# Causal squares of the row-maximum pass: a GpSimd select in place of a mask matmul

## The chip, the cores and the metric

One core of a Trainium2 chip runs the whole kernel. The metric is the device time of one execution in microseconds (us); the kernel before took 1416.82 us, the median of three runs. The engines are TensorE (PE; its weight loads are PEld), VectorE (DVE), ScalarE (ACT), GpSimd (POOL) and SyncE (SP), which here only issues DMAs. Each works through its own queue of instructions in order, and a wait at the head of a queue holds everything behind it.

## The reference, cut to what matters

One decoder layer over 2048 tokens of width 1024: `x + W_out(concat(A, B, C) * silu(z))`, where A is latent attention (8 heads), B differential attention (4 heads, two softmax maps each) and C attention to 256 memory tokens. A and B are causal:

```python
sc = jnp.einsum('bqhd,bkhd->bhqk', qblk, k).astype(jnp.float32) * scale
sc = jnp.where(causal_mask(start, s)[None, None], sc, NEG_INF)
p = jax.nn.softmax(sc, axis=-1)
```

A softmax may subtract any number near the row's maximum before the exponential, since it cancels in the quotient. The kernel computes a row maximum of the masked scores beforehand and carries it into the scores as one more row of the contraction.

## The kernel before, in words

The 2048 queries are cut into 4 blocks of 512 (b = 0 to 3), each of 4 row tiles of 128. The work is a list of 28 steps: 4 of the memory branch, 8 of the differential branch (2 groups of heads x 4 blocks), 16 of the latent branch (4 groups x 4 blocks). A step has a preparation (`prep_d`, `prep_a`: projections, norms and rotary embedding, keys and queries split into fp16 pairs and transposed by DMA), then the row-maximum pass `est_block`, then its maps (class `Map`): for each tile of 128 keys the scores with keys on the partitions (L546, or L890 to L892, with a mask product at L549 or L894 for the diagonal tile), the exponential p on ACT (L492), the low part plo on DVE (L493), and the products with the values on PE (L502, L504, L505).

`est_block` (L373) is where the change is. For each map m, row tile t and key block c up to b it makes on PE the scores of 128 queries (on the partitions) against up to 512 keys (L384, tile pe, one of three PSUM banks). In the query's own block, c == b, only the first t + 1 squares of 128 keys are computed, and the last of these, on the diagonal, gets the causal mask by a second product at L386, identity times `mask_e`, which adds -1e30 above the diagonal into the same bank. How the maximum is then taken depends on `fold`, true for b of 1 or more:

- Block 0: DVE reduces the bank directly (L388, tile mx).
- Blocks 1 to 3: ACT copies the first key block from PSUM to a bf16 tile er (L390; one buffer, holding two row tiles) and each later one to a bf16 tile ec (L393; three buffers). DVE takes the elementwise maximum of er and ec (L394). After each pair of row tiles DVE halves er three times (L398) and reduces the rest (L399).

Then DVE writes the scaled maxima into the query stack (L407), and SP issues the DMA that transposes the queries again with the maxima in them (L470, L873), which releases the maps. In blocks 1 to 3 the diagonal square always passes through an ec, never through er.

POOL, beside the memsets of the stacks (L448, L853, L859), computes the norms: an addition (L97) and a power of -1/2 (L101, tiles r_d, r_a, yr_d), the rotary tables (L318 to L321), and in the latent branch the rotary embedding of the queries (L340 to L344), the last of which DVE's L845 and L848 need. POOL issues one DMA, at the start; all others are SP's.

A loop at the end of the kernel (from L1176) decides in which order steps, fills (gates, latents, output projection) and maps are written down, from planned costs and due times; preparation and `est_block` get a priority 200 behind that of the maps. The tile framework then makes each engine's queue from these priorities and a modelled timeline, anew at each build:

```python
with tile.TileContext(nc, schedule_with_timeline_sim=True) as tc:
```

Of the kernel before, what the change touches and what calls it, by code (L numbers as in the profile page):

```python
# [16 lines left out]
ALU = mybir.AluOpType  # L17
AX = mybir.AxisListType

P = 128  # L20
# [4 lines left out]
NK = DM // P  # L25
EPS = 1e-6
NEG = -1.0e30
WS = 64.0
# [12 lines left out]
def hybrid_block(ctx: ExitStack, tc: tile.TileContext, x, mem, positions, norm_g, w_in, mla_q_norm_g,  # L41
# [3 lines left out]
    V, A, G, T, SP = nc.vector, nc.scalar, nc.gpsimd, nc.tensor, nc.sync  # L45
# [15 lines left out]
    def bigt(shape, name):  # L61
        return big.tile(shape, F16, tag="big", name=name)

# [1 line left out]
    ident = cst.tile([P, P], BF16, name="ident")  # L65
    make_identity(nc, ident)
    mask_t = cst.tile([P, P], BF16, name="mask_t")
# [33 lines left out]
        G.tensor_tensor(rv, rv, m.broadcast_to([P] + list(shape)), ALU.pow)  # L101
        return rv

# [1 line left out]
    def stage(name, pool=None):  # L105
        if pool is big:
            return big.tile([P, DM], F32, tag="big", name=name)
# [6 lines left out]
    PACE, NPACE = 6, 6  # L114

    def load(dst, src, pace=PACE):
        """At the start, loads take turns with the transposes on the DMA queues."""
        if 0 < len(turned) < 2 * NPACE:
            with tc.issue_after(turned[max(0, len(turned) - pace)].ins):
                SP.dma_start(dst, src)  # L120
        else:
            SP.dma_start(dst, src)
# [16 lines left out]
        turned.append(SP.dma_start_transpose(ht[:, 1], lo))  # L139
        return ht  # L140

# [1 line left out]
    def load_w(w, cols, gains, name, out, pool=None, ahead=2, pace=PACE):  # L143
        """Column ranges of w as fp16 pairs: NK views [P, 2, n] appended to out."""
        n = sum(c for _, c in cols)
        kpu = 2 if n > 256 else 4

        def fetch(i):
            st = stage(f"wst_{name}{i}", pool).rearrange("p (k c) -> p k c", k=2)
            at = 0  # L150
            for c0, c in cols:
                load(st[:, :, at:at + c], w[0, 2 * i * P:(2 * i + 2) * P, c0:c0 + c].rearrange("(k p) c -> p k c", p=P), pace)
                at += c
            return st

        sts = [fetch(i) for i in range(ahead - 1)]
        yield 1.0
        for i in range(NK // 2):
            if i + ahead - 1 < NK // 2:
                sts.append(fetch(i + ahead - 1))  # L160
                yield 1.0
            st = sts[i]
            if 2 * i % kpu == 0:
                wt = bigt([P, kpu, 2, 1024 // kpu], f"w_{name}{i}")
            for k in range(2):
                g = gains[:, 2 * i + k:2 * i + k + 1]
                dst = wt[:, (2 * i + k) % kpu]
                A.activation(dst[:, 0, :n], st[:, k, :n], AF.Copy, scale=g)
                V.scalar_tensor_tensor(dst[:, 1, :n], st[:, k, :n], g, dst[:, 0, :n], ALU.mult, ALU.subtract)
                out.append(dst)  # L170
            yield 1.0
# [6 lines left out]
            T.matmul(ps[:, :n], lhsT=ht[:, 1, k], rhs=wt[:, 0, :n], start=False, stop=(k == NK - 1))  # L178

    def project_block(hts, units, n, dst):  # L180
        """dst: [P, 4, >= n]"""
        for t in range(4):
            ps = ps_p.tile([P, 512], F32, tag="pp", name="pp")
            project(ps, hts[t], units, n)
            A.activation(dst[:, t, 0:n], ps[:, :n], AF.Copy, scale=1.0 / WS)
            yield 0.01 * n
# [4 lines left out]
    def tmp4(name):  # L191
        return wk.tile([P, 1024], F32, tag="t4", name=name, bufs=2)

# [1 line left out]
    top = tc.cur_priority  # L195
    tc.cur_priority = top + 1000
    g_mk = gain_row(mem_kn_g, 64, "g_mk")
# [46 lines left out]
        mem_left.clear()  # L244
        yield 1.0

# [1 line left out]
    cos_t = cst.tile([P, NT, 16], F32, name="cos_t")  # L248
    sin_t = cst.tile([P, NT, 16], F32, name="sin_t")

# [59 lines left out]
    tc.cur_priority = top  # L310

    def rope_tabs(b, g, name):
        """cos and sin of block b's tokens with the halves of the gain folded in."""
        tb = wk.tile([P, 2, 4, 32], F32, tag="rtab", name=f"rt_{name}", bufs=1)
        c = cos_t[:, 4 * b:4 * b + 4, :]
        s = sin_t[:, 4 * b:4 * b + 4, :]
        g1, g2 = _bc(g[:, 0:16], 1, 4), _bc(g[:, 16:32], 1, 4)
        G.tensor_tensor(tb[:, 0, :, 0:16], c, g1, ALU.mult)  # L318
        G.tensor_tensor(tb[:, 0, :, 16:32], c, g2, ALU.mult)
        G.tensor_tensor(tb[:, 1, :, 0:16], s, g2, ALU.mult)  # L320
        G.tensor_tensor(tb[:, 1, :, 16:32], s, g1, ALU.mult)  # L321
        return tb

    def rope(dst, src, tb, nh, eng, name):
        """dst, src: [P, 4, nh, 32]"""
        tmp = tmp4(f"rtmp_{name}")[:, 0:128 * nh].rearrange("p (t h d) -> p t h d", t=4, d=32)
        C = _bc(tb[:, 0], 2, nh)
        Sn = _bc(tb[:, 1], 2, nh)
        eng.tensor_tensor(dst, src, C, ALU.mult)
        eng.tensor_tensor(tmp[..., 0:16], src[..., 16:32], Sn[..., 0:16], ALU.mult)  # L330
        eng.tensor_tensor(tmp[..., 16:32], src[..., 0:16], Sn[..., 16:32], ALU.mult)
        eng.tensor_tensor(dst[..., 0:16], dst[..., 0:16], tmp[..., 0:16], ALU.subtract)
        eng.tensor_tensor(dst[..., 16:32], dst[..., 16:32], tmp[..., 16:32], ALU.add)

    def rope_in_place(q, tb, nh, eng, tmp):
        """q: [P, 4, nh, 32]"""
        tmp = tmp.rearrange("p (t h d) -> p t h d", t=4, d=32)
        C = _bc(tb[:, 0], 2, nh)
        Sn = _bc(tb[:, 1], 2, nh)
        eng.tensor_tensor(tmp[..., 0:16], q[..., 16:32], Sn[..., 0:16], ALU.mult)  # L340
        eng.tensor_tensor(tmp[..., 16:32], q[..., 0:16], Sn[..., 16:32], ALU.mult)
        eng.tensor_tensor(q, q, C, ALU.mult)
        eng.tensor_tensor(q[..., 0:16], q[..., 0:16], tmp[..., 0:16], ALU.subtract)
        eng.tensor_tensor(q[..., 16:32], q[..., 16:32], tmp[..., 16:32], ALU.add)  # L344

# [1 line left out]
    zsc = dr.tile([3, P, NT, 2 * P], F32, name="zsc")  # L347
    part = dr.tile([P, NT, DM], F32, name="part")
    ysc = dr.tile([P, NB, 8, 1024], F16, name="ysc")
# [1 line left out]
    hts = []  # L351

    def put_v(vt, ps):
        """vt: [P, 2, 130], ps: [P, 2, 64] in PSUM, WS times the values"""
        A.activation(vt[:, :, 0:64], ps, AF.Copy, scale=1.0 / WS)
        V.scalar_tensor_tensor(vt[:, :, 65:129], ps, 1.0 / WS, vt[:, :, 0:64], ALU.mult, ALU.subtract)

    def put_gate(z, ps):
        """2 WS silu of the products ps"""
        A.activation(z, ps, AF.Tanh, scale=0.5 / WS)  # L360
        V.scalar_tensor_tensor(z, z, 1.0, ps, ALU.add, ALU.mult)

# [6 lines left out]
    class Step:  # L369
        pass  # L370

# [1 line left out]
    def est_block(st, i, nmap, mcol, lhs, rhs):  # L373
        b = st.b
        mx = sm.tile([P, nmap, 4, 2], F32, tag="mx", name=f"mx{i}_{st.name}", bufs=2)
# [1 line left out]
        for m in range(nmap):  # L377
            for t in range(4):
                if fold and t % 2 == 0:
                    er = wk.tile([P, 2, 512], BF16, tag="er", name="er", bufs=1)  # L380
                for c in range(b + 1):
                    ps = ps_e.tile([P, 512], F32, tag="pe", name="pe")
                    n = (4 if c < b else t + 1) * P
                    T.matmul(ps[:, 0:n], lhsT=lhs(m, t), rhs=rhs(m, c, n // P), start=True, stop=c < b)  # L384
                    if c == b:
                        T.matmul(ps[:, t * P:n], lhsT=ident, rhs=mask_e, start=False, stop=True)  # L386
                    if not fold:
                        V.reduce_max(mx[:, m, t, c:c + 1], ps[:, 0:n], axis=AX.X)  # L388
                    elif c == 0:
                        A.activation(er[:, t % 2], ps, AF.Copy)  # L390
                    else:
                        ec = wk.tile([P, 512], BF16, tag="ec", name="ec", bufs=3)
                        A.activation(ec[:, 0:n], ps[:, 0:n], AF.Copy)  # L393
                        V.tensor_tensor(er[:, t % 2, 0:n], er[:, t % 2, 0:n], ec[:, 0:n], ALU.max)  # L394
                    yield 0.5
                if fold and t % 2:
# [9 lines left out]
        for m in range(nmap):  # L406
            V.tensor_scalar_mul(mcol(m), mr[:, m, :], -1.0 / MS)  # L407

# [1 line left out]
    def prep_d(st, units):  # L410
        g, b, nm = st.g, st.b, st.name
        qk = new_qkv(f"qkv_{nm}")[:, :, 0:256]
# [59 lines left out]
            yield 1.0  # L472

    class Map:
        """One softmax map of one block of queries."""

        def __init__(self, scale, scores, vtile, njt, diag0, unit, done):
            self.scale, self.scores, self.vtile, self.njt, self.diag0 = scale, scores, vtile, njt, diag0
# [35 lines left out]
        return wk.tile([P, 2, 4, P], F16, tag="ys", name=f"ys{ct}_{b}", bufs=1)  # L514

    def finish(st, y, ct, ys, keep=False):
        """y: [P, 4, 128], already gated; its fp16 parts go out transposed."""
        b = st.b
        A.activation(ys[:, 0], y, AF.Copy)
        yield 1.0  # L520
# [10 lines left out]
    last = {}  # L531
# [48 lines left out]
        yield 1.0  # L580
        yield from finish(st, yf, 4 + st.g, ys)

# [1 line left out]
    def prep_m(st, units):  # L584
        b, nm = st.b, st.name
        qkv = new_qkv(f"qkv_{nm}")[:, :, 0:256]
# [82 lines left out]
        yield 1.0  # L669
        yield from finish(st, yf, ct, new_ys(ct, st.b), keep=st.name == steps[-1].name)  # L670

# [1 line left out]
    def gates(b, chunk, units):  # L673
        """2 WS silu(z) of two groups for one block, kept in DRAM."""
        for t in range(4):
            ps = ps_p.tile([P, 512], F32, tag="pp", name="pp")
            project(ps, hts[4 * b + t], units, 256)
# [3 lines left out]
            SP.dma_start(zsc[chunk, :, 4 * b + t, :], zt)  # L681
            yield 2.6

# [1 line left out]
    krot, ss_kr = [], []  # L685
    z_left = [0, 1]
    lat_left = [0, 1]
# [64 lines left out]
            SP.dma_start(lq_d[:, b, :], lt.rearrange("p a k -> p (a k)"))  # L752
        lat_left.remove(1)

# [1 line left out]
    wuq, wukv = [], []  # L756
    lat_q, lat_kv = [], []

# [142 lines left out]
                            1.0, done))  # L901
        return maps

# [1 line left out]
    wout = {}  # L905

    def load_wout(cs):
# [13 lines left out]
        return yt  # L921

    def out_tile(yt, t, hf, acc):
        """Adds the product of the given channel tiles to one [128, 512] tile of acc."""
        ps = ps_p.tile([P, 512], F32, tag="pp", name="pp")
        tk = slice(P * t, P * t + P)
        o = slice(512 * hf, 512 * hf + 512)
# [5 lines left out]
        V.scalar_tensor_tensor(acc, ps, 0.5 / WS, acc, ALU.mult, ALU.add)  # L933

    def out_dm():
        """x plus the products of the differential and memory channels, kept in DRAM."""
        yield from load_wout(range(4, 8))
        for b in range(NB):
            yield from await_y(b, range(4, 8))
# [27 lines left out]
    HELD = 4  # L967

    def out_last():
        """All but the last channel tile for the last block, kept on chip."""  # L970
        b = NB - 1
        yield from await_y(b, range(0, 3))
        y01 = y_pair(b, 0)
# [27 lines left out]
                out_tile([(3, y3)], t, hf, acc[:, o])  # L1001
                SP.dma_start(out[0, P * i:P * i + P, o], acc[:, o])

# [1 line left out]
    zcol = 1440  # L1005
    d_cols = [[(416 + 128 * g, 128), (672 + 128 * g, 128), (928 + 128 * g, 128), (zcol + 512 + 128 * g, 128)]
              for g in range(2)]
# [228 lines left out]
```

## Time and profile before

| | |
|---|---|
| median of three runs | 1416.82 us (1413.11 to 1417.91) |
| span of the profiled execution | 1420.8 us; the page lists no other time for it |
| mean granted TensorE clock | 0.982 |
| PE busy | 1312.4 us, 92% |
| DVE busy | 1120.2 us, 79% |
| ACT busy | 897.6 us, 63% |
| POOL busy | 359.8 us, 25% |

The profile is of one execution. Busy times of PE are modelled, because matmuls overlap: a matmul's duration includes the way through the array, and the next one starts long before it ends. A line such as L386 is the line of the kernel that made the instruction. "x192" counts instructions. A wait is named by who waited and for whom.

### The profile page before, as it was taken

The numbers are of one execution on the slowest core, as the hardware profiler recorded it, in microseconds if no ns is written. First come the engines' busy times: TensorE is split into PE (matmuls) and PEld (weight loads), VectorE is DVE, ScalarE is ACT, GpSimd is POOL, SyncE is SP. The second block draws the span as 40 slices with busy tenths as digits, with TensorE's granted clock in tenths as the row PEclk, the third lists the DMA queues.
The fourth block names the chain that finished last, engine by engine and source line by source line (L and its number), as shares of the span: only waits on it lengthen the run. The fifth ranks groups of instructions, "written<-read, shape, count | busy, mean of one in ns | idle before, by whom it ended". The sixth has DMA issues, their size and how long they took to land. (4 is left out here: it accounts for less than half of the span.)

```text
span 1420.8 us, 35214 instructions
## 1 busy us (share of the span) xinstructions
PE 1312.4 (92%) x13552; PEld 831.7 (59%) x13552; DVE 1120.2 (79%) x2649; ACT 897.6 (63%) x2153; POOL 359.8 (25%) x541
## 2 busy tenths in 40 slices
PE   4789899999999999998998999999999899989998
PEld 1344456667676666677775665655655565555554
DVE  3458787889789958888899788977788999975645
ACT  5646444677777747786776676655776788664521
POOL 2222133303052044122321233533124433200000
PEclk9899999999999999999999999999999999999999
DMA  8999754223223223347245156255544454264352
GB/s 211 244 211 196 162 111 100 53 66 69 52 53 76 39 35 64 68 123 196 97 98 134 50 153 167 57 127 125 110 87 87 105 94 75 54 142 153 113 204 78
DMA packets 302696, 157.67 MB, mean 111 GB/s; under 512 B 248384, under 2 KB 281280, under 8 KB 302528
## 3 DMA queue, kind: packets, MB, share of 16 engines
q1 hardware_dynamic: 302496, 155.42, 47.6%
q8 instruction: 106, 1.74, 0.5%
q14 instruction: 62, 0.51, 0.1%
q0 software_dynamic: 32, 0.00, 0.0%
HBM read 61.79 MB, written 34.34 MB: 68 GB/s over the span
## 5 line engine op out<-in xcount | busy, mean ns | idle before, releaser
L492 ACT ACTIVATE p<-st 128x512 f32<-128x512 f32 (+3 forms) x672 | 354.6, 547 | 177.6 <-PE st L892 60.5
L493 DVE TENSOR_TENSOR plo<-p 128x512 f16<-128x512 f32 (+3 forms) x672 | 407.5, 617 | 60.1 <-ACT p L492 56.0
L505 PEld LDWEIGHTS <-plo 128*128 128x128 f16 x2304 | 217.5, 99 | 52.1 <-DVE plo L493 31.8
L502 PEld LDWEIGHTS <-p 128*128 128x128 bf16 x2304 | 219.1, 98 | 49.0 <-issue 2.3
L504 PEld LDWEIGHTS <-p 128*128 128x128 bf16 x2304 | 218.2, 98 | 29.4 <-issue 0.6
L393 ACT ACTIVATE ec<-pe 128x512 bf16<-128x512 f32 (+3 forms) x384 | 196.3, 537 | 40.5 <-PE pe L386 18.8
L394 DVE TENSOR_TENSOR er<-er,ec 128x512 bf16<-128x512 bf16 (+3 forms) x384 | 143.6, 380 | 33.5 <-ACT ec L393 20.4
L502 PE MATMUL pv<-V_d,p 128*128 128x65 f16 x1088 | 140.8, 193 | 0.8 <-DVE y_d L557 0.8
L504 PE MATMUL pv<-V_d,p 128*128 128x64 f16 x1088 | 140.7, 195 | 0.0
L502 PE MATMUL pv<-V_a,p 128*128 128x65 f16 x1088 | 139.4, 194 | 0.2
L504 PE MATMUL pv<-V_a,p 128*128 128x64 f16 x1088 | 139.2, 195 | 0.0
L505 PE MATMUL pv<-V_d,plo 128*128 128x65 f16 x1088 | 134.8, 192 | 4.5 <-DVE plo L493 3.9
L505 PE MATMUL pv<-V_a,plo 128*128 128x65 f16 x1088 | 130.6, 193 | 8.5 <-DVE plo L493 7.9
L390 ACT ACTIVATE er<-pe 128x512 bf16<-128x512 f32 x192 | 109.6, 604 | 38.3 <-DVE mx_d L399 14.2
L176 PEld LDWEIGHTS <-ht_x 128*128 128x128 f16 x896 | 88.5, 99 | 70.9 <-DMA ht_x<-xh_x 20.2
L890 PE MATMUL st<-qB_a,kT_a 97*128 97x512 f16 (+1 forms) x320 | 112.1, 350 | 18.0 <-ACT p L492 17.2
L177 PEld LDWEIGHTS <-ht_x 128*128 128x128 f16 x896 | 88.4, 99 | 55.5 <-issue 9.3
L178 PEld LDWEIGHTS <-ht_x 128*128 128x128 f16 x896 | 88.4, 99 | 54.5 <-DMA ht_x<-xl_x 4.6
L546 PE MATMUL st<-qB_d,kT_d 97*128 97x512 f16 (+1 forms) x320 | 109.2, 349 | 9.1 <-ACT p L492 8.3
L384 PE MATMUL pe<-kT_d,qB_d 96*128 96x512 f16 (+2 forms) x320 | 106.0, 350 | 8.2 <-ACT ec L393 4.7
L891 PE MATMUL st<-qB_a,kT_a 96*128 96x512 f16 (+1 forms) x320 | 112.0, 350 | 0.0
L892 PE MATMUL st<-qB_a,kT_a 96*128 96x512 f16 (+1 forms) x320 | 111.4, 348 | 0.0
(285 smaller groups left out, 3383.9 us busy)
## 6 DMA issues: line engine op xcount, KB each, us to landing
xt_x<-in_x_dram SPq DMA_DIRECT2D x16, 512.0 KB, 4.6
xr<-in_x_dram SPq DMA_DIRECT2D x16, 512.0 KB, 3.6
part<-xr SPq DMA_DIRECT2D x16, 512.0 KB, 3.0
ysc<-yt SPq DMA_DIRECT2D x31, 256.0 KB, 2.2
yl<-ysc SPq DMA_DIRECT2D x15, 512.0 KB, 4.3
zsc<-zc SPq DMA_DIRECT2D x48, 128.0 KB, 2.3
xa<-part SPq DMA_DIRECT2D x12, 512.0 KB, 3.6
out_dram<-xa SPq DMA_DIRECT2D x12, 512.0 KB, 2.7
```

What stands on the lines that cost most here:

```text
L390: A.activation(er[:, t % 2], ps, AF.Copy)
L393: A.activation(ec[:, 0:n], ps[:, 0:n], AF.Copy)
L394: V.tensor_tensor(er[:, t % 2, 0:n], er[:, t % 2, 0:n], ec[:, 0:n], ALU.max)
L492: A.activation(p32[:, :n], ps[:, :n], AF.Exp, scale=self.scale)
L493: V.tensor_tensor(plo[:, :n], p32[:, :n], phi[:, :n], ALU.subtract)
L502: T.matmul(pvv[:, t, 0:65], lhsT=phi[:, c], rhs=vt[:, 0:65], start=(j == 0 and t == 0), stop=False, skip_group_check=True)
L504: T.matmul(pvv[:, t, 0:64], lhsT=phi[:, c], rhs=vt[:, 65:129], start=False, stop=False, skip_group_check=True)
L505: last["pv"] = T.matmul(pvv[:, t, 0:65], lhsT=plo[:, c], rhs=vt[:, 0:65], start=False, stop=(j == self.njt - 1), skip_group_check=True)
L546: T.matmul(ps[:, :n], lhsT=st.kTs[j // 4][0:97, h, j % 4, m % 2, :], rhs=st.qB[h][0:97, t0:4, m % 2, :], start=True, stop=not diag)
L890: T.matmul(ps[:, :n], lhsT=kt[0:97, h, j % 4, 0, :], rhs=q[0:97, 0, t0:4, :], start=True, stop=False)
L891: T.matmul(ps[:, :n], lhsT=kt[0:96, h, j % 4, 0, :], rhs=q[0:96, 1, t0:4, :], start=False, stop=False)
L892: T.matmul(ps[:, :n], lhsT=kt[0:96, h, j % 4, 1, :], rhs=q[0:96, 0, t0:4, :], start=False, stop=not diag)
```

## The change

In blocks 1 to 3 the mask product at L386 is left out, so the score product is the only one of its group. After ACT has copied the own block's scores to ec, GpSimd overwrites the part of the last square above the diagonal with -1e30 in the bf16 copy, in place (an affine select keeps an element where row index minus column index is at least 0 and fills the others), and DVE's maximum then waits for GpSimd. Block 0 keeps the product. The other hunks of the diff only blank out comments and docstrings, with the line numbers kept.

```diff
@@ def est_block(st, i, nmap, mcol, lhs, rhs)
-                    T.matmul(ps[:, 0:n], lhsT=lhs(m, t), rhs=rhs(m, c, n // P), start=True, stop=c < b)
-                    if c == b:
+                    T.matmul(ps[:, 0:n], lhsT=lhs(m, t), rhs=rhs(m, c, n // P), start=True, stop=fold or c < b)
+                    if c == b and not fold:
                         T.matmul(ps[:, t * P:n], lhsT=ident, rhs=mask_e, start=False, stop=True)
...
                         ec = wk.tile([P, 512], BF16, tag="ec", name="ec", bufs=3)
                         A.activation(ec[:, 0:n], ps[:, 0:n], AF.Copy)
+                        if c == b:
+                            G.affine_select(ec[:, t * P:n], ec[:, t * P:n], pattern=[[-1, P]], base=0,
+                                            channel_multiplier=1, compare_op=ALU.is_ge, fill=NEG)
                         V.tensor_tensor(er[:, t % 2, 0:n], er[:, t % 2, 0:n], ec[:, 0:n], ALU.max)
```

## Rows read from the trace of the kernel before

**Rows 1.** Page of the profile, parts 1 and 2: span, busy time.

```profile
span 1420.8 us, 35214 instructions
...
PE 1312.4 (92%) x13552; PEld 831.7 (59%) x13552; DVE 1120.2 (79%) x2649; ACT 897.6 (63%) x2153; POOL 359.8 (25%) x541
```

**Rows 2.** Windows of the block-attention stretches (columns in the first line).

```profile
core 0: us, PE busy (x) PEld busy (x) DVE busy (x) ACT busy (x) POOL busy (x), PEclk, DMA share, GB/s
210.00:745.00 535.00, 515.90 (x5773) 363.75 (x5772) 447.50 (x1170) 375.46 (x973) 142.11 (x175) 0.99 0.36 80
745.00:1345.00 600.00, 553.50 (x6168) 348.53 (x6165) 502.83 (x1174) 396.62 (x951) 165.24 (x256) 0.98 0.47 107
```

**Rows 3.** Page, part 4: the chain that ended last, shares by engine.

```profile
PE 23%; DMA 6%; DVE 6%; POOL 4%; ACT 3%; issue 2%; ACTq 0%; SPq 0%; POOLq 0%; DVEq 0%
```

**Rows 4.** Lines by shape: ACT copies of one block, DVE reductions of pairs of tiles.

```profile
L390 ACT ACTIVATE er<-pe 128x512 bf16<-128x512 f32 x192 | 109.6, 604 | 38.3 <-DVE mx_d L399 14.2 <-DVE mx_a L399 12.0 <-PE pe L384 8.8
...
L399 DVE TENSOR_REDUCE mx_d<-er 128x2 f32<-128x128 bf16 x48 | 13.4, 280 | 0.7
```

**Rows 5.** Line L386, the mask product: duration ns min/median/max, first and last start.

```profile
L386 PE MATMUL pe<-mask_e,ident x256: 217/219/314, 208.2 to 1334.3; 128*128 128x128 bf16 x128
```

**Rows 6.** Timeline of PE around one mask product (start us, us, what).

```profile
401.44 0.22 PE L386 MATMUL pe<-mask_e,ident 128*128 128x128 bf16 x1
401.50 0.19 PE L505 MATMUL pv<-V_d,plo 128*128 128x65 f16 x1
```

**Rows 7.** Lines of POOL by shape (busy us, mean ns, idle before).

```profile
L101 POOL TENSOR_TENSOR r_a<-r_a,mhalf 128x16 f32<-128x16 f32 x16 | 48.6, 3039 | 0.5
L101 POOL TENSOR_TENSOR r_d<-r_d,mhalf 128x32 f32<-128x32 f32 x8 | 44.5, 5557 | 0.7
...
masks.py:30 POOL TENSOR_SCALAR_AFFINE_SELECT mask_e<-mask_e 128x128 bf16<-128x128 bf16 x1 | 0.3, 282 | 0.0
```

**Rows 8.** Lines L97, L318 and L394: duration ns min/median/max.

```profile
L97 POOL TENSOR_SCALAR r_a<-ss_a x16: 259/400/718, 701.4 to 1225.8; 128x16 f32<-128x16 f32 x16
...
L318 POOL TENSOR_TENSOR rt_a<-cos_t,g_q x16: 315/547/2307, 647.3 to 1202.1; 128x64 f32<-128x64 f32 x16
...
L394 DVE TENSOR_TENSOR er<-er,ec x384: 208/415/949, 246.9 to 1335.6; 128x512 bf16<-128x512 bf16 x121, 128x128 bf16<-128x128 bf16 x38, 128x384 bf16<-128x384 bf16 x33
```

**Rows 9.** Waits, all engines: us in total, times, longest us.

```profile
PEld L505 <- DVE plo L493: 31.8, 59, 2.5
...
DVE er L394 <- ACT ec L393: 20.4, 32, 2.5
...
DVE kn_a L845 <- POOL r_a L101: 17.7, 13, 3.5
...
PE st L890 <- ACT p L492: 17.2, 22, 1.8
...
ACT er L390 <- DVE mx_d L399: 14.2, 15, 2.8
...
ACT er L390 <- DVE mx_a L399: 12.0, 15, 1.7
...
PE pv L505 <- DVE plo L493: 11.8, 17, 2.0
...
PE st L546 <- ACT p L492: 8.3, 17, 2.0
...
PE pe L384 <- DMA qB_a<-qs_a: 6.5, 6, 2.2
```

**Rows 10.** Timelines of two row-maximum passes beside the power operation.

```profile
319.29 5.44 POOL L101 TENSOR_TENSOR r_d<-r_d,mhalf 128x32 f32<-128x32 f32 x1
...
320.51 0.47 ACT L393 ACTIVATE ec<-pe 128x384 bf16<-128x384 f32 x1
...
1026.72 3.10 POOL L101 TENSOR_TENSOR r_a<-r_a,mhalf 128x16 f32<-128x16 f32 x1
...
1026.56 0.40 ACT L393 ACTIVATE ec<-pe 128x128 bf16<-128x128 f32 x1
```

## The prediction, made before the changed kernel was run

> **What bounds the kernel now.** The page's busy line comes first: PE is busy for 1312.4 of 1420.8 us, DVE for 1120.2, ACT for 897.6, POOL for 359.8 [rows 1]. A busy PE is a modelled figure, so the second view is the windows of the two stretches in which the row-maximum pass of blocks 1 to 3 runs. In the differential stretch (210 to 745 us) PE is busy for 515.90 of 535 us, in the latent one (745 to 1345 us) for 553.50 of 600, with DVE at 447.50 and 502.83 [rows 2]. PE sets the pace in the first; in the second it also does for nine tenths of the time, and the rest are holes. The third view, the chain that ended last, agrees: PE has the largest share, 23%, and DMA, DVE and POOL have 6, 6 and 4% [rows 3]. The waits then tell how late work elsewhere reaches PE: PE's weight loads and matmuls waited 31.8 and 11.8 us for plo from DVE, and its scores 17.2 and 8.3 us for ACT to free a bank [rows 9]. All profile sums below are made against the 1420.8 us span; the page gives no other time for that execution, and it is 4.0 us (0.3%) above the 1416.82 us median of the runs.
>
> **How many.** L390 copies the first block of keys of every row tile of a folded query block, 192 times; one mask product belongs to each, 192 of the 256 at L386 [rows 4, 5]. The other 64 are of block 0 and stay. Half of the 192 lie in each stretch: there are 48 pair reductions on the differential side and, by the 192, as many on the other [rows 4].
>
> **Removed: 192 mask products.** A duration of 219 ns is latency [rows 5]; what PE gets back is the slot, from a product's start to the next one's: 401.44 to 401.50, 0.06 us [rows 6]. 192 x 0.06 = 11.5 us. Where PE is idle anyway a slot is worth nothing, so I weigh each half by PE's busy share: 96 x 0.06 x 0.964 + 96 x 0.06 x 0.923 = 10.9 us gained [rows 2]. Bounds: 11.5 and 0. The identity's weight load goes too; it runs beside matmuls and is already in the slot.
>
> **Added: 192 selects on POOL.** The same operation on the same 128x128 bf16 shape ran three times at the start of the kernel, one of them in 282 ns [rows 7], with nothing beside it. In mid-kernel POOL's operations are stretched: a one-input operation has minimum 259 and median 400 ns [rows 8], 0.14 us more. So 0.28 + 0.14 = 0.42 us each, 81 us in all, and POOL goes from 25 to about 31% of the span [rows 1]: cover enough, so the busy time itself costs nothing. What can cost is what waits behind it, in four terms. To turn a wait on DVE into time I use the share that reaches PE today: DVE stood still for 1420.8 - 1120.2 = 301 us, PE waited 31.8 + 11.8 = 43.6 us for it, 0.145 [rows 1, 9]; for ACT (17.2 + 8.3) / 523 = 0.05.
>
> The first term is the longer way from ACT's copy to DVE's maximum. DVE waited for the copy in 32 of 384 cases [rows 9], so about 16 of the 192 masked squares have no cover at all: 16 x 0.42 x 0.145 = 1.0 us; bounds nothing, and 2.0 if all 32 stood at masked squares. Behind the maximum on DVE's queue stand the plo subtractions that PE needs.
>
> The second is the single er buffer. ACT's next pair waits until the pair is reduced, 15 + 15 times today [rows 9], and each of these may end 0.42 us later: 30 x 0.42 x 0.05 = 0.6 us; bounds nothing, and 2.0 if all 96 pairs end in such a wait. The three ec buffers are held 0.42 us longer as well; that falls under the same price. The PSUM banks are freed by the copy as before.
>
> The third is POOL's own queue. The power operation of the next step's norm takes 5.56 or 3.04 us [rows 7], and both passes that I looked at had copies of scores ending inside one [rows 10]. A select queued behind it comes late, and the maximum with it. The order does not allow for that length: DVE's kn_a waited for this operation 13 times, 17.7 us, 1.36 us each [rows 9]. There are 18 folded steps (6 and 12); I take two thirds with such a meeting: 12 x 1.36 x 0.145 = 2.4 us; bounds nothing, and the last rival below. In the other direction the select waits in order for ACT's copy, and behind it on POOL stand the next step's rope tables, memsets and norms, which have 69% of POOL's time free; I cost that at nothing. Without that cover it would show as longer waits of kn_a for POOL.
>
> The fourth is DVE beside POOL. The same maximum takes 208 to 949 ns with a median of 415, and a POOL table of 315 ns took up to 2307 [rows 8]: the two engines hold each other up. I let half of the selects hold DVE for half of their 0.28 us: 192 x 0.5 x 0.14 = 13 us of DVE, x 0.145 = 2.0 us. Bounds: nothing, and the rival below. SP's queue and all DMAs are untouched.
>
> **Sum.** -10.9 + 1.0 + 0.6 + 2.4 + 2.0 = -4.9 us. From the median: 1416.8 - 4.9 = 1411.9, so **1412 us**, 0.34% faster. A measurement of this kernel can tell about 0.3%, 4.2 us, from no change; the forecast lies just beyond it. The order of every queue is made anew when the program is built, so small waits will also move about; I allow 5 us either way, about the spread of the three runs shown.
>
> **Rivals.** *The two engines exclude each other fully.* Then every select waits for the subtraction or maximum in front and holds the next one for its whole 282 ns: 192 x 0.282 = 54 us of DVE, and x 0.145 the fourth term is 7.9 us instead of 2.0. Sum: +1.0, 1418 us, no change. For it: the 2307 and the 949 ns [rows 8]; against it: the median of 415 ns is near the shorter waits, so most operations today meet nobody. The Trainium skill's page "SBUF — State Buffer", section "Who interferes with whom", states this rule: a DVE instruction with two SBUF inputs contends with a GpSimd instruction that reads SBUF, and the second to issue fully blocks. By that rule the change would be worth nothing; the trace agrees that such operations stretch, not that each one does. Chance 0.15.
>
> *The latent half gains nothing.* There PE has holes of 46.5 us [rows 2], and its row-maximum products wait for the transposed queries (6.5 us, 6 times [rows 9]): a slot freed ahead of such a wait only lengthens it. Then the gain is 5.5 us, the costs stay at 6.0: 1417 us, no change. For it: the DMA share of the chain; against it: PE is still busy for 92% of that stretch. Chance 0.17.
>
> *POOL's queue takes the place of the product.* One select behind each power operation waits half of it, 6 x 2.8 + 12 x 1.5 = 35 us, and DVE, which works in order, stands still with it. If that reaches PE not at 0.145 but at 0.6, the sum is -10.9 + 21 = +10, 1427 us, slower. It decides from a share of 10.9 / 35 = 0.3. For it: the copies that end inside a power operation [rows 10]; against it: the single waits of PE for plo are at most 2.5 us, and DVE has other work in 79% of the time. Chance 0.25 for this side.
>
> **Chances and range.** Forecast 0.43, the two that end within 0.3% together 0.32, the slower one 0.25. The low end is the full 11.5 us less the smallest costs (nothing), with 3 us for the new order: 1402. The high end takes in the slower rival: 1428. Between forecast and no change the likeliest range is 1406 to 1419.
>
> **What would show it.** L386 with 64 matmuls; 192 selects with a median near 0.4 us; PE's busy time about 11 us less if the modelled time follows the slot (more, if the latency tail of 0.2 us shows); PE's waits for plo up by 2 to 6 us. Wrong for the first rival: the maxima's median well above 415 ns. Wrong for the third: DVE's waits for the selects over 30 us in total, single ones of 2 us and more, with the power operation running. If POOL's norms come later, kn_a's wait grows from 17.7 us. The forecast falls if PE's busy time drops and the span does not follow.

## The result, and the profile after

The changed kernel takes **1439.49 us**, median of four runs (1435.98 to 1440.52), against 1416.9 us for the kernel before beside it (1413.11 to 1417.91): 1.0156 times as long, interval 1.0135 to 1.0177. Slower by 22.6 us, where 1412 us and a gain were forecast, and above the range's upper end of 1428 us. The profiled execution took 1438.58 us.

Its span and clock, as the list of the cores gives them:

```profile
core 0: 1436.9 us, clock 0.977
```

The page: busy times of the engines, the shares of the chain that ended last, and the groups of the select and of the maximum behind it (sum in us, mean ns of one | idle time before it and what ended most of it).

```profile
PE 1313.7 (91%) x13360; PEld 820.8 (57%) x13360; DVE 1128.5 (79%) x2649; ACT 897.9 (62%) x2153; POOL 442.9 (31%) x733
...
PE 45%; DVE 16%; DMA 15%; issue 8%; ACT 7%; POOL 6%; SPq 2%; POOLq 0%; ACTq 0%; DVEq 0%
...
L395 POOL TENSOR_SCALAR_AFFINE_SELECT ec<-ec 128x128 bf16<-128x128 bf16 x192 | 90.3, 472 | 382.1 <-ACT ec L393 372.9
L397 DVE TENSOR_TENSOR er<-er,ec 128x512 bf16<-128x512 bf16 (+3 forms) x384 | 146.5, 387 | 50.9 <-POOL ec L395 27.0
```

Against [rows 1], PE has 192 matmuls fewer and is busy no less (1312.4 before), DVE for 8.3 us more, POOL for 83.1 us more. PE's idle time went from 1420.8 - 1312.4 = 108.4 us to 1436.9 - 1313.7 = 123.2 us. The chain now covers nearly the whole span instead of 44% [rows 3]; as the chain of the kernel without any mask (below, faster than before) has 53% PE, its shares say nothing of the loss.

The windows of the two stretches (columns as in [rows 2]) show where PE lost:

```profile
210.00:745.00 535.00, 515.96 (x5667) 357.86 (x5664) 449.17 (x1157) 373.68 (x963) 178.85 (x271) 0.99 0.36 79
745.00:1345.00 600.00, 539.12 (x5917) 334.30 (x5916) 496.42 (x1157) 389.60 (x941) 210.47 (x350) 0.97 0.46 104
```

In the differential stretch PE is as busy as before, 515.96 against 515.90 us, and gets through 106 matmuls fewer (x5773 before), 96 masks among them at most; in the latent one its holes grew from 46.5 to 60.9 us.

The select's durations (ns: shortest/median/longest) from the answer on its line, and the waits that answer to [rows 9] (us in total, times, longest):

```profile
L395 POOL TENSOR_SCALAR_AFFINE_SELECT ec<-ec x192: 283/320/3175, 245.8 to 1353.2; 128x128 bf16<-128x128 bf16 x192
```

```profile
POOL ec L395 <- ACT ec L393: 372.9, 118, 20.6
...
PEld L508 <- DVE plo L496: 46.7, 87, 3.4
...
DVE er L397 <- POOL ec L395: 27.0, 52, 3.0
...
ACT er L390 <- DVE mx_d L402: 20.4, 19, 2.4
...
PE pv L508 <- DVE plo L496: 18.9, 35, 3.3
...
ACT er L390 <- DVE mx_a L402: 16.8, 14, 2.7
...
DVE kn_a L848 <- POOL r_a L101: 13.3, 9, 2.6
...
ACT ec L393 <- DVE er L397: 13.0, 11, 3.4
...
DVE er L397 <- ACT ec L393: 9.4, 15, 2.2
```

ACT's wait for a free ec buffer in the kernel before, which [rows 9] do not have:

```profile
ACT ec L393 <- DVE er L394: 3.9, 6, 1.0
```

DVE has a new wait of 27.0 us for POOL in place of 11.0 us of its wait for ACT (20.4 to 9.4). 118 of the 192 selects found POOL idle and began when ACT's copy was done. ACT's wait for a free ec buffer went from 3.9 to 13.0 us, and PE's two lines of waiting for plo from 43.6 to 65.6 us. These two overlap, because a weight load and the matmul behind it each count the same standstill (1.69 and 1.20 us at 987.06 in the pass below). The matmuls alone went from 11.8 to 18.9 us, while the score matmuls' waits for ACT's p fell from 25.5 [rows 9] to 18.8 us (15.6 at L893, 3.2 at L549). kn_a waits less than before, so POOL's own norms did not become late.

**One pass, before and after.** The same row-maximum pass of the latent branch in the two timelines (start, duration, engine, line; in brackets the idle time before and who ended it). Before:

```profile
962.63 0.43 PE L384 MATMUL pe<-kT_a,qB_a 96*128 96x512 f16 x2
...
963.79 0.28 ACT L393 ACTIVATE ec<-pe 128x128 bf16<-128x128 f32 x1
...
964.66 0.21 DVE L394 TENSOR_TENSOR er<-er,ec 128x128 bf16<-128x128 bf16 x1
...
969.52 0.27 DVE L399 TENSOR_REDUCE mx_a<-er 128x2 f32<-128x128 bf16 x1
...
976.26 0.22 DVE L407 TENSOR_SCALAR qs_a<-mx_a 128x4 f16<-128x4 f32 x1
```

After:

```profile
977.92 0.65 PE L384 MATMUL pe<-kT_a,qB_a 96*128 96x512 f16 x3
...
979.09 0.28 ACT L393 ACTIVATE ec<-pe 128x128 bf16<-128x128 f32 x1
...
981.96 3.37 POOL L101 TENSOR_TENSOR r_a<-r_a,mhalf 128x16 f32<-128x16 f32 x1
...
985.31 0.28 POOL L395 TENSOR_SCALAR_AFFINE_SELECT ec<-ec 128x128 bf16<-128x128 bf16 x1
...
985.37 0.77 DVE L848 TENSOR_TENSOR kn_a<-kn_a,r_a 128x512 f32<-128x512 f32 x1 [2.20 <-POOL r_a L101]
...
986.93 0.48 DVE L397 TENSOR_TENSOR er<-er,ec 128x128 bf16<-128x128 bf16 x1
...
987.06 0.10 PEld L508 LDWEIGHTS <-plo 128*128 128x128 f16 x1 [1.69 <-DVE plo L496]
987.06 0.20 PE L508 MATMUL pv<-V_a,plo 128*128 128x65 f16 x1 [1.20 <-DVE plo L496]
...
987.50 0.60 ACT L393 ACTIVATE ec<-pe 128x512 bf16<-128x512 f32 x1 [2.99 <-DVE er L397]
...
988.63 0.38 PE L893 MATMUL st<-qB_a,kT_a 97*128 97x512 f16 x1 [1.03 <-ACT p L495]
...
989.28 0.76 POOL L321 TENSOR_TENSOR rt_a<-sin_t,g_q 128x64 f32<-128x64 f32 x1
...
990.00 0.54 POOL L395 TENSOR_SCALAR_AFFINE_SELECT ec<-ec 128x128 bf16<-128x128 bf16 x2
...
995.03 0.28 DVE L402 TENSOR_REDUCE mx_a<-er 128x2 f32<-128x128 bf16 x1
...
995.34 1.09 ACT L390 ACTIVATE er<-pe 128x512 bf16<-128x512 f32 x2 [2.18 <-DVE mx_a L402]
...
1000.60 0.17 DVE L410 TENSOR_SCALAR qs_a<-mx_a 128x4 f16<-128x4 f32 x1
```

From the copy of the first diagonal square to the start of its maximum it is 0.87 us before, 7.84 us after: the select stands behind the next step's embedding and its power operation of 3.37 us (starting 6.22 us after the copy), and the maximum then behind DVE's own work for another 1.3 us. All three ec buffers are then taken, so ACT's next copy waits 2.99 us, and ACT works in order: exponentials of the maps stand behind that copy, and PE waits for p (1.03 us). PE's wait for plo (1.20 us) has another reason: DVE's queue has kn_a in front of that plo and of the maximum, and kn_a waits 2.20 us for the same power operation. So this pass does not show the select's delay alone. Two more selects wait behind the rotary tables. The pass took 976.48 - 962.63 = 13.9 us and now takes 1000.77 - 977.92 = 22.9 us.

PE's granted clock falls in this pass. The windows (columns as in [rows 2]) of the whole pass before, then of two stretches of the pass after:

```profile
962.63:976.48 13.85, 13.85 (x159) 8.50 (x158) 12.36 (x28) 10.99 (x25) 7.01 (x15) 1.00 0.69 188
```

```profile
985.80:989.96 4.16, 1.45 (x17) 0.69 (x17) 4.07 (x6) 1.57 (x3) 4.16 (x6) 1.00 0.44 126
989.97:993.37 3.40, 3.40 (x30) 1.96 (x31) 3.05 (x6) 1.19 (x2) 2.02 (x7) 0.50 0.02 5
```

Before, PE was busy throughout and kept the upper of its two levels (2.4 GHz, 1.00). After, it was busy for 1.45 of 4.16 us while it waited for plo and p, and then had the lower level (1.2 GHz, 0.50) for 3.40 us of full work.

DVE's longest single wait for a select, in the timeline of after around 867 us:

```profile
866.83 0.31 POOL L862 MEMSET qs_a<- 128x256 f16 x1 [5.70 <-DMA qB_a<-qs_a]
867.09 0.29 POOL L395 TENSOR_SCALAR_AFFINE_SELECT ec<-ec 128x128 bf16<-128x128 bf16 x1
...
867.42 0.54 DVE L397 TENSOR_TENSOR er<-er,ec 128x256 bf16<-128x256 bf16 x1 [3.02 <-POOL ec L395]
...
869.74 0.20 PE L508 MATMUL pv<-V_a,plo 128*128 128x65 f16 x1 [3.27 <-DVE plo L496]
```

Here POOL was idle: a memset of a query stack, waiting 5.70 us for a DMA, stood in front of the select. The plo that PE needs is made behind the late maximum, and PE stands still for 3.27 us.

Most waits of DVE for a select have no queue behind them. In the timeline 39 of the 52, with 18.2 of the 27.0 us, are for a select that began as soon as its copy was done, as this one (part of such a wait is the one for the copy itself):

```profile
605.96 0.60 ACT L393 ACTIVATE ec<-pe 128x512 bf16<-128x512 f32 x1 [1.35 <-PE pe L384]
...
606.63 0.29 POOL L395 TENSOR_SCALAR_AFFINE_SELECT ec<-ec 128x128 bf16<-128x128 bf16 x1 [1.92 <-ACT ec L393]
...
606.95 0.42 DVE L397 TENSOR_TENSOR er<-er,ec 128x512 bf16<-128x512 bf16 x1 [1.62 <-POOL ec L395]
```

58 of the 192 selects began more than 0.3 us after their copy, 28 of them with a power operation in between. In most of these cases DVE had other work: it did not stand still, but the maximum came late and the buffers were held. From the end of a diagonal square's copy to the start of its maximum it is 2.32 us on average before and 3.33 us after.

### The profile page after: what moved, and what is told of

It reads as the page before. It is cut to its first block, busy times and chain, and to the rows that moved or that the text cites. A ratio compares the mean times of both kernels' runs of the same rounds, so it can differ in the third digit from the quotient of the medians.

```text
span 1436.9 us, 35457 instructions
## 1 busy us (share of the span) xinstructions
PE 1313.7 (91%) x13360; PEld 820.8 (57%) x13360; DVE 1128.5 (79%) x2649; ACT 897.9 (62%) x2153; POOL 442.9 (31%) x733
## 4 chain that ended last, share of the span: by engine, by line
PE 45%; DVE 16%; DMA 15%; issue 8%; ACT 7%; POOL 6%; SPq 2%; POOLq 0%; ACTq 0%; DVEq 0%
PE pp L178 5%; PE pp L176 5%; PE pp L177 5%; DVE plo L496 5%; PE pe L384 4%; DMA qB_a<-qs_a 4%; DMA kT_a<-ks_a 3%; PE pp L933 3%; PE pp L934 3%; PE pp L935 3%; PE pv L508 3%; PE st L549 3%; PE pv L507 2%; PE pv L505 2%; PE st L893 2%
## 5 line engine op out<-in xcount | busy, mean ns | idle before, releaser
L395 POOL TENSOR_SCALAR_AFFINE_SELECT ec<-ec 128x128 bf16<-128x128 bf16 x192 | 90.3, 472 | 382.1 <-ACT ec L393 372.9
L397 DVE TENSOR_TENSOR er<-er,ec 128x512 bf16<-128x512 bf16 (+3 forms) x384 | 146.5, 387 | 50.9 <-POOL ec L395 27.0
L390 ACT ACTIVATE er<-pe 128x512 bf16<-128x512 f32 x192 | 109.3, 607 | 48.7 <-DVE mx_d L402 20.4
L893 PE MATMUL st<-qB_a,kT_a 97*128 97x512 f16 (+1 forms) x320 | 112.0, 350 | 17.9 <-ACT p L495 15.6
L549 PE MATMUL st<-qB_d,kT_d 97*128 97x512 f16 (+1 forms) x320 | 111.0, 355 | 5.4 <-ACT p L495 3.2
L894 PE MATMUL st<-qB_a,kT_a 96*128 96x512 f16 (+1 forms) x320 | 111.8, 349 | 0.0
```

The source lines that it names most:

```text
L549: T.matmul(ps[:, :n], lhsT=st.kTs[j // 4][0:97, h, j % 4, m % 2, :], rhs=st.qB[h][0:97, t0:4, m % 2, :], start=True, stop=not diag)
```

## The experiments

Ratios are to the kernel before, run beside them on the same chip, with 95% intervals. Two explanations stood against each other at first: the stage on POOL that the maximum now passes through, and the new order of the queues alone. Then the stage was taken apart: its length, what it reads, who waits for it.

**Each part alone.** The kernel with neither product nor select (the mask is left out of the row maxima, and the exponent is scaled by 0.25):

```diff
-                        if c == b:
-                            G.affine_select(...)
-            A.activation(p32[:, :n], ps[:, :n], AF.Exp, scale=self.scale)
+            A.activation(p32[:, :n], ps[:, :n], AF.Exp, scale=0.25 * self.scale)
```

> Leaves the causal mask out of the row-maximum pass of blocks 1 to 3 (no product, no select) and scales the exponent by a quarter so that the wrong maxima do no harm; otherwise as the changed kernel. Theory A (the select's lateness on POOL, passed on by DVE and ACT, costs more than the product did): the 192 slots come back, 1404 to 1410 us. Theory B (the queues were made anew, and any new order of this size costs about as much as the change did): slower than before here too, 1425 us or more.

Measured: 0.9977 [0.9963, 0.9991], 1415.82 us, between the ranges of both theories. Its page and its clock:

```profile
PE 1306.6 (92%) x13360; PEld 819.9 (58%) x13360; DVE 1120.5 (79%) x2649; ACT 898.4 (64%) x2153; POOL 365.2 (26%) x541
...
PE 53%; DVE 14%; DMA 12%; POOL 8%; ACT 7%; issue 5%; SPq 2%; ACTq 0%; DVEq 0%; POOLq 0%
```

```profile
core 0: 1414.8 us, clock 0.978
```

In this order the removal is worth 0.2%, about 3 us, not 10.9, and PE's busy time fell by 5.8 us, not 11. Over the ten runs of this kernel the mean granted clock was 0.977 (0.974 to 0.982), over the thirteen of the kernel before beside it 0.984 (0.981 to 0.987). One minus the clock, times the span, is the PE time lost below full clock: 32.1 against 23.2 us. So up to 8.9 of the 11.5 us of freed slots are offset by a lower clock. The changed kernel has 0.975 on average in its four runs, which by the same working is at most 12 of its loss of 22.6 us. Why the clock is lower is not shown. Missing matmuls are not needed for it: three kernels below that have all 13552 show 0.975 to 0.977 (product and select at lead 11.3, the side select at 11.3, and the own block first with the product). A kernel in which only the exponent is scaled was not run, so what that does by itself is open too.

Product and select together (before, plus the three lines of the select):

> The kernel before with the select added behind the copy, and the mask product kept. Theory A: the cost of the select alone, about 11 us above the changed kernel, 1445 to 1455 us. Theory B: no more than the changed kernel's loss and not tied to it, 1420 to 1440 us.

Measured: 1.0178 [1.0159, 1.0197], 1444.56 us, just below Theory A's range. The select by itself costs 1444.56 - 1420.04 = 24.5 us (1420.04 is the kernel before beside it); with the product taken out as well it is 1.0156. The two parts about add.

Only one kind of step changed (`sel = fold and nmap == 2` in place of `fold` for the differential steps, `nmap == 1` for the latent ones):

> The change in the differential branch alone (96 selects); the latent branch keeps its products. Theory A: the loss stays away, since the changed kernel was level with the one before at 766 us: 1410 to 1418 us. Theory B: slower by 10 us or more, since all queues are made anew from there on as well.

> The change in the latent branch alone (96 selects); the differential branch keeps its products. Theory A: nearly the whole loss, 1434 to 1446 us. Theory B: a loss of no set size, anywhere from 1415 to 1440 us.

Measured: 1.0065 [1.0042, 1.0088], 1429.37 us, and 1.0097 [1.008, 1.0114], 1432.47 us. Each half loses, and the sum, 1.62%, is about the whole. Theory A, which put nearly all of the loss into the latent branch, missed both.

**Another order.** The planner's lead (`LEAD = 11.0`) sets when passes are written down. With 10.7 and 11.3 both kernels get other queues, with the same instructions:

> The kernel before with the planner's LEAD at 10.7 instead of 11.0: the same instructions in another order, for the size of what a new order alone does. Theory A: within 6 us of before, either way. Theory B (a new order costs as much as the change did): slower by 10 us or more.

> The kernel before with LEAD at 11.3. Theory A: within 6 us of before, either way. Theory B: slower by 10 us or more.

> The changed kernel with LEAD at 10.7. Theory A: the loss against its twin of the kernel before stays, 15 to 28 us. Theory B: the loss against its twin changes freely and may be gone.

> The changed kernel with LEAD at 11.3. Theory A: 15 to 28 us above its twin of the kernel before. Theory B: any difference, also none.

Measured, before: 0.9995 [0.9976, 1.0014] and 0.991 [0.9886, 0.9934], the second 13 us faster, which neither theory had; after: 1.0141 [1.0119, 1.0164] and 1.0129 [1.0107, 1.0151]. The new order alone is not the cause: the change loses 1.5 points at 10.7, 1.6 at 11.0 and 2.2 at 11.3. The last is 31 us, more than Theory A's 15 to 28. But an order by itself moves the kernel by up to 0.9%, more than the forecast effect; the kernel before with 11.3 (1405.44 us, span 1403.7 us at clock 0.987) beats both kernels of this case by that one number.

**The mask on DVE** (`V.tensor_tensor(ec[:, t*P:n], ec[:, t*P:n], mask_e, ALU.add)` in place of the select), no POOL in it:

> The mask made by DVE instead of POOL: an in-place addition of the mask to the last square of ec, ahead of the maximum on the same queue (192 more DVE instructions of about 0.22 us, 42 us). If the loss comes from waiting for a third engine or from POOL's queue (theories A1, A2), it is mostly gone: 1410 to 1424 us. If any lengthening of the pass on DVE's side costs as much, 1432 us or more.

Measured: 1.0097 [1.007, 1.0123], 1432.24 us, DVE busy for 1146.7 us. Half a per cent better than POOL's select, although it loads DVE with 18.2 us more than the select kernel; still a loss, in the range for "any lengthening of the pass". A loss of six tenths of the size (0.97 of 1.56 points) thus comes without any POOL in the pass.

**A select nobody's maximum waits for** (product kept, the select writes a tile that nobody reads):

```diff
...
+                        if c == b:
+                            es = wk.tile([P, P], BF16, tag="es", name="es")
+                            G.affine_select(es, ec[:, t * P:n], ...)
```

To make room for es, three small tiles of the rotary tables at the start of the kernel are laid into its buffer.

> The kernel before, product kept, with the 192 selects reading ec and writing a tile that nobody reads: POOL is as full, waits as long for ACT, holds ec and meets DVE at the port, but no maximum waits for it. Theory A1 (POOL's queue standing before the selects delays the next step's norms, or the port): the loss of the run with both, 1436 to 1448 us. Theory A2 (the maximum's wait at the head of DVE's queue): close to before, 1415 to 1425 us.

> Product kept, the select written aside so that no maximum waits for it, LEAD 11.3. If POOL's side costs 12 us whatever the order: 0.998 to 1.002 of before. If the wait of DVE is all of it and the first run of this kind only caught a bad order: 0.988 to 0.994.

Measured: 1.0083 [1.0056, 1.0111], 1429.73 us, between the two ranges, and 1.0142 [1.0118, 1.0166] at lead 11.3, above both. The waits at the ec buffers in the first:

```profile
ACT ec L394 <- POOL es L397: 8.2, 8, 2.3
ACT ec L394 <- DVE er L399: 7.5, 10, 1.5
```

So there is a loss in both orders though no maximum waits for a select. An ec buffer is not free until POOL has read it, and ACT waits for it (15.7 us in all, 3.9 before). That this wait makes the loss is likely and not shown.

**The own block first.** ACT copies the query block's own scores first, and their maximum is taken last, after those of the other key blocks, so the select has time; the control does the same with the mask product:

```diff
-                for c in range(b + 1):
+                for c in [b] + list(range(b)) if fold else range(b + 1):
...
+                        if c == b - 1:
+                            V.tensor_tensor(er[:, t % 2, 0:nd], er[:, t % 2, 0:nd], ed[:, 0:nd], ALU.max)
```

> The changed kernel with the own block taken first in each row tile and its maximum last, so that a select has the time of one to three other blocks before DVE needs it. Theory A2: most of the loss is gone, 1408 to 1422 us. Theory A1: it stays, 1432 us or more.

> The control for the run above: the kernel before with the same turn of the loop, product kept. Both theories: within 10 us of before, either way, as for any new order.

Measured: 1.0091 [1.0057, 1.0126], 1431.38 us, with the select, and 1.0057 [1.003, 1.0083], 1425.56 us, with the product. The first is far above Theory A2's range and just below Theory A1's; the control is within its 10 us. DVE's wait for POOL in the first:

```profile
DVE er L397 <- POOL ec L392: 2.9, 6, 1.6
```

27.0 us of waiting became 2.9, and the change's loss against its control is 0.34 points instead of 1.56, though POOL does the same work; the intervals of the two overlap, so it may be nothing. In this one order most of the loss goes when the masked copy need not be ready at once. Against the kernel before little is won, as the new order costs 0.57% itself, and the side select loses without such a wait.

**Both parts at lead 11.3**, to have a second order for each:

> As the run without any mask in the pass (product and select left out in blocks 1 to 3, exponent scaled by a quarter), from the order with LEAD 11.3, whose kernel with the product took 0.991 of before. Theory A: 4 to 11 us below that twin, 0.983 to 0.988 of before. If the new order decides: anywhere from 0.98 to 1.00.

> Product and select, LEAD 11.3. Theory A: 20 to 30 us above the twin, 1.005 to 1.012 of before; the changed kernel at LEAD 11.3 was at 1.013. If the new order decides: not tied to 25 us.

Measured: 0.998 [0.9962, 0.9998] and 1.0163 [1.0137, 1.0189], both above Theory A's ranges, so the order decides part of either size. At 11.3 the kernel without any mask is slower than the one with all products (0.991). Over ten runs its clock is 0.977 again, and the four runs of that fast kernel have 0.985.

**A shorter stage, and one that reads nothing.** In place of the select POOL zeroes the square with a memset; the long one zeroes 448 columns. The own block's scores are lost in both, and the exponent is scaled by 0.05.

```diff
-                            G.affine_select(ec[:, t * P:n], ec[:, t * P:n], ...)
+                            G.memset(ec[:, t * P:n], 0.0)      (long: ec[:, 0:448])
```

> The changed kernel with the select replaced by a memset of the whole last square of ec to zero (the square's scores are lost, and the exponent is scaled by 0.05 so that this does no harm): the same waits before and behind it, but POOL reads nothing. If the meeting of POOL's reads with DVE's operands is the cause: 1418 to 1426 us. If the waits are: 1430 to 1442 us.

> As the run with the short memset, but over 448 columns of ec (about 0.47 us, the select's mean; the own block's scores are lost, the exponent is scaled by 0.05). If POOL's reads meeting DVE's operands are the cause: as with the short memset, 1.002 to 1.006 of before. If the time until POOL is done is the cause, whatever it does: 1.012 to 1.018, as with the select.

> The short memset with LEAD 11.3; the changed kernel there took 1.0129 of before, its twin without the change 0.991. If the short memset's gain is real: 0.999 to 1.007. If it was the order's: 1.010 or more.

Measured: short 1.0041 [1.0017, 1.0064], 1425.43 us, in the range for POOL's reads as the cause; long 1.0151 [1.0117, 1.0185], in the range for the time until POOL is done; short at lead 11.3 1.01 [1.0065, 1.0135], at the edge of the range in which the gain of the first was the order's. The durations on the memset's line, the short one's first, then the long one's with DVE's wait for it:

```profile
L395 POOL MEMSET ec<- x192: 196/204/206, 247.5 to 1343.5; 128x128 bf16 x192
```

```profile
L395 POOL MEMSET ec<- x192: 462/471/507, 248.8 to 1352.2; 128x448 bf16 x192
```

```profile
DVE er L396 <- POOL ec L395: 27.7, 35, 1.9
```

A memset of 471 ns, about the select's mean of 472, costs what the select costs although it reads no SBUF and its duration hardly varies. Reading SBUF at the same moment as DVE is thus not needed for a loss of this size. It need not be the same loss, though. The long memset's four runs have a mean clock of 0.969 and the short one's ten have 0.980; by the working above 44.9 and 28.9 us are lost below full clock, and this difference of 16 us is as large as that of the times (14.5 us). The short memset's own runs differ likewise, from 1418.58 us at 0.983 to 1429.99 us at 0.975. The short one costs less in its first order, and its two orders differ by 0.6 points.

All pairs that have both orders, as ratios at lead 11.0, 11.3 and their mean:

| kernel | 11.0 | 11.3 | mean |
|---|---|---|---|
| before | 1 | 0.991 | 0.9955 |
| neither product nor select | 0.9977 | 0.998 | 0.9979 |
| after | 1.0156 | 1.0129 | 1.0143 |
| product and select | 1.0178 | 1.0163 | 1.0171 |
| select to the side, product kept | 1.0083 | 1.0142 | 1.0113 |
| short memset, no product | 1.0041 | 1.01 | 1.0071 |

With the order averaged that far, the select as a stage on POOL costs 1.6 points (after less neither) or 2.2 (both less before); taking the product out gives 0.3 with the select there, and nothing measurable without.

## Why the prediction was wrong

The third rival had the sign; the forecast took it as a small term. That rival's sum also leaves out the other three costs of 3.6 us: with them it gives +13.7 us, about 1430 us, above the range that was to take it in. Step by step:

- **How many: right.** 192 selects, 192 matmuls fewer.
- **The gain, -10.9: mis-sized.** It measured about -3 us alone (0.9977) and also about -3 us beside the select (1.0178 to 1.0156). At lead 11.3 it was about +10 us alone (0.991 to 0.998). Weighing the slots by PE's busy share left out that PE's granted clock can change: 32.1 us were lost below full clock instead of 23.2. Whether the clock or the order takes the gain was not isolated.
- **The select's price, 0.42 us: right in the middle, short in the tail.** Median 0.32, mean 0.47 us, longest 3.2.
- **The first term, the longer way to the maximum, +1.0: too few waits.** 16 x 0.42 = 6.7 us of DVE's waits were forecast; 39 waits with 18.2 us stood at selects that had no queue in front, 11 of these us after the copy was done.
- **The third term, POOL's queue, +2.4: the queue is there, but DVE waits less behind it than forecast.** 12 x 1.36 = 16 us were forecast. The trace has 28 selects behind a power operation, more than the 12, but DVE mostly had other work. The 13 waits that were not for a select that began at once sum to 8.8 us, 3.0 of them behind a memset that waited for a DMA. The rival's mark ("over 30 us in total, single ones of 2 us and more, with the power operation running") was not reached.
- **The share of 0.145, the price in every cost: this is the step that failed.** The first and third terms had 6.7 + 16.3 = 23 us of DVE's waits, and 27.0 were measured. At 0.145 these are 3.9 us; the select alone cost 24.5 us (1444.56 against 1420.04), and all four cost terms together had 6.0. The share averages over all of DVE's idle time, and its 43.6 us count in part the same standstill twice, at the weight load and at the matmul. The longest wait of DVE, 3.02 us, reached PE as 3.27.
- **The second term, +0.6: the step that priced the ec buffers with the er pair, at 0.05.** ACT's waits for ec and er together went from 3.9 + 14.2 + 12.0 = 30.1 us to 13.0 + 20.4 + 16.8 = 50.2 us. The side select, in which no maximum waits for POOL, goes with a loss of 0.8 to 1.4%.
- **The clock: no term at all.** At most 12 of the 22.6 us of loss go with it.
- **The fourth term and the first rival, DVE beside POOL: the engines meet, but that is not needed for the loss.** DVE was busy for 8.3 us more, forecast 13; the maximum's mean went from 380 [rows 8 have its median] to 387 ns and its median from 415 to 414. The Trainium skill's page "SBUF — State Buffer", section "Who interferes with whom", says that a DVE instruction with two SBUF inputs contends with a GpSimd instruction that reads SBUF, and not with one that only writes it. The trace agrees that meetings stretch the select: the 42 that overlap no two-input operation of DVE take at most 294 ns, others up to 3175, while the memset that reads nothing stays at 196 to 206. But the long memset costs as much without the meeting.
- **POOL's later work behind the select at nothing: right.** kn_a's wait fell from 17.7 to 13.3 us.
- **The allowance of 5 us for a new order: too small.** Orders of the same instructions gave -0.9% (lead 11.3) to +0.6% (the own block first), 13 us one way and 8 the other.

What stays open: DVE's waits for POOL do not rank the kernels by themselves (24.0 us for the short memset at 1.0041, 27.7 for the long one at 1.0151), nor does any other single wait. That the select costs 1.5 to 2.2 points is shown in several orders; how the loss splits between DVE's waits, ACT's buffers and the clock, and what lowers the clock, is not. More than three ec buffers were not tried.

## What to carry to other kernels

A new stage in a pass is not free because its engine is idle for most of the time: most of DVE's waits here were for selects with no queue in front of them. The queue adds to that, so look at its longest instructions and at those that wait for a DMA. The average share of an engine's waits that reaches the bottleneck is no price for a new wait on the way of a short-buffered chain: follow one pass, count its buffers, and look at the granted clock where the bottleneck stood still. And where a planner makes the order anew, compare each variant with its twin in several orders before 1% is put down to an edit.

## What was not expected of the hardware

The same select took from 283 to 3175 ns with a median of 320, while a memset on the same square stayed within 196 to 206 ns in 192 executions. And kernels that differ little have different mean granted clocks: 0.984 before, 0.977 without any mask in ten runs at either lead, 0.980 with the short memset and 0.969 with the long one, each a mix of the levels of 1.2 and 2.4 GHz. Between the two memsets this is as large as the difference in time.
